# Modulation rows of a hybrid transformer layer: partial sums in four column groups of TensorE

## The chip, the core and the metric

The kernel runs on one core of one Trainium2 chip. A core has four engines that compute, each with a queue of its own that is worked through in order: TensorE (PE in the profile; PEld is its weight load), VectorE (DVE), ScalarE (ACT) and GpSimd (POOL). SyncE (SP) issues the DMA transfers of this kernel, apart from the gathers, which POOL issues. TensorE reads SBUF and writes PSUM, of which there are eight banks of 128 partitions by 512 fp32 values. The metric is the device time of one execution in microseconds (us).

## What is computed

One layer on 512 latent tokens and 256 context tokens of width 1024: a modulated layer norm, a mixing sublayer (windowed attention beside a bidirectional gated delta rule), a second modulated norm, and a product-key retrieval of experts (PEER). The change touches the modulation alone:

```python
mod   = silu(c)     @ w_ada + b_ada          # latent: 6 vectors of 1024
mod_c = silu(c_ctx) @ w_ada + b_ada          # context: the first two are used
sh1, sc1, gt1, sh2, sc2, gt2 = split(mod, 6)
h  = standardize(x) * (1 + sc1) + sh1        # hc likewise, with mod_c
x  = layer_norm(ALPHA * x + gt1 * mixing(h, hc), ln1_g, ln1_b)
h  = standardize(x) * (1 + sc2) + sh2
x  = layer_norm(ALPHA * x + gt2 * peer(h), ln2_g, ln2_b)
```

w_ada is 1024 x 6144 in fp32, 24 MB, so it is read once in full: 24 transfers of 1 MB (half of the 1024 rows, as four k-tiles of 128, by 512 columns).

## The kernel before

The program is written by a planner. Each piece of work is a generator (t_ada1, t_hT, t_qkv, t_prep and so on) that yields, ahead of each instruction, the engine and an estimated duration (p16, p32, dv, ac, pl, dm, lines 164 to 189). The Driver (lines 67 to 153) keeps a time for each engine and emits, among the tasks that could start first, the one with the lowest priority number; it sets the order of every engine's queue. The priorities are in the table X (line 196). A `later` step does not hold its task back. Buffers (SBUF slots, PSUM banks) are taken from and given back to pools, with get and put; seven PSUM banks are one pool (pj, under several names), and the eighth (obk) is another.

The modulation is done in two halves.

The **first half**, t_ada1 (line 506), makes shift and scale of the first norm, for latent and context tokens. For each of four column tiles (ct) and two halves (hf) a 1 MB tile of w_ada is loaded, and four products of a 128x2 stationary operand (silu of c and c_ctx) with 128x512 fp32 values accumulate into two rows of a bank (line 541). The task turn adds the bias on DVE (line 516) and turns the rows into columns with four PE transposes (line 521). When all 16 columns are there, they are copied to modT (lines 549, 551), and t_hT (line 631), which waits for modT, may modulate the transposed tokens (ACT line 643 and DVE line 649) and split them into two fp16 parts (lines 654, 657). All projections read these.

The **second half**, t_ada2 (line 561), makes the four rows for latent tokens that are used later (gt1, sh2, sc2, gt2). Its priority is 9.268, behind the projections of keys, values and queries (3.2 to 6.2) and ahead of the z projections (11.34). It has three slots of SBUF for its 16 loads. It doesn't use TensorE for the sum over the k-tiles: a k-tile is 128 partitions by 512 columns, each partition has one multiplier, and the eight k-tiles are summed elementwise first. Even k-tiles go through DVE (line 611 for the first, 613 after it), odd ones are scaled on ACT (line 604) and added on POOL (lines 607, 617). Then one product with a column of ones sums over the 128 partitions (line 584, in bank obk), DVE adds the bias (line 586), and the row is stored to DRAM (line 590). A column tile ct waits for the store of ct - 2.

When the second half has ended (ev_ada2), the delta rule's recurrence t_chain and its loads t_vin, the attention (t_att0), and two more sets of working buffers become possible, since they use the memory of these slots or read the rows. Before that stand the projections (t_qkv, t_ka, t_qa, t_z: 21 weight tiles of w_in, split into two fp16 parts by ACT line 701 and DVE line 703), the convolution (DVE lines 857 and 860) and the preparation of the delta rule's chunks, t_prep. After the recurrence and the attention follow the output projection t_out (line 1577; its last DVE step on the product is line 1597), and the PEER part: queries (t_q, with DVE line 1802 on its weights), selection and gate matrices (DVE lines 1857 to 2029), and the expert products, which fill TensorE to the end.

## Time and profile before

| | us |
|---|---|
| median of three runs | 1718.34 (1718.12 to 1723.7) |
| profiled execution, its own time | 1715.12 |
| its span, first to last instruction | 1713.3 |

| stretch of the span, us | what runs |
|---|---|
| 0 to 40 | loads, first half of the modulation, statistics of the tokens |
| 40 to 58 | modulated and transposed tokens |
| 58 to 252 | projections, convolution, second half of the modulation, first chunks of the delta rule; the first step of the recurrence on DVE stands at 251.4 |
| 252 to 530 | recurrence, remaining chunks, attention, output projection |
| 530 to 836 | queries of PEER, selection, gate matrices, first expert products |
| 836 to 1713 | expert products |

A busy time is the union of an engine's instructions in a stretch. In the lists by line a group has its count, its busy time and the mean duration of one; durations of neighbours overlap on DVE, ACT and PE, so that busy time by count is nearer to what one more instruction takes. Where an instruction waited, the profile names what ended the wait. The chain of waits follows back from the last instruction to whatever released each one; its shares by line tell on what the end depended. An fp32 product of 512 columns leaves two records on PE, one after the other.

### The profile page before, as it was taken

The numbers are of one execution on the slowest core, as the hardware profiler recorded it, in microseconds if no ns is written. First come the engines' busy times: TensorE is split into PE (matmuls) and PEld (weight loads), VectorE is DVE, ScalarE is ACT, GpSimd is POOL, SyncE is SP. The second block draws the span as 40 slices with busy tenths as digits, with TensorE's granted clock in tenths as the row PEclk, the third lists the DMA queues.
The fourth block names the chain that finished last, engine by engine and source line by source line (L and its number), as shares of the span: only waits on it lengthen the run. The fifth ranks groups of instructions, "written<-read, shape, count | busy, mean of one in ns | idle before, by whom it ended". The sixth has DMA issues, their size and how long they took to land.

```text
span 1713.3 us, 29275 instructions
## 1 busy us (share of the span) xinstructions
PE 1624.7 (95%) x10971; PEld 984.9 (57%) x10971; DVE 1483.8 (87%) x2905; ACT 818.0 (48%) x1475; POOL 530.8 (31%) x383
## 2 busy tenths in 40 slices
PE   8889899888998999999999999999999999989997
PEld 2554466787856885677655555555555555534443
DVE  5789985887899999999987789888888988898976
ACT  2645769777543434566543333333333333344441
POOL 0423451433002000000005455555445545554100
PEclk9999999999999999999999999999999999999999
DMA  9546322222134403599989999999999999999852
GB/s 360 185 156 206 120 75 69 77 66 67 41 133 142 142 2 99 159 271 278 276 302 332 355 353 361 365 375 341 361 381 338 369 361 332 328 344 335 327 182 74
DMA packets 157170, 404.41 MB, mean 236 GB/s; under 512 B 12498, under 2 KB 71378, under 8 KB 151906
## 3 DMA queue, kind: packets, MB, share of 16 engines
q1 hardware_dynamic: 120164, 268.30, 45.5%
q0 software_dynamic: 36864, 134.23, 21.4%
q8 instruction: 86, 1.41, 0.3%
q14 instruction: 56, 0.46, 0.1%
HBM read 365.84 MB, written 36.65 MB: 235 GB/s over the span
## 4 chain that ended last, share of the span: by engine, by line
PE 58%; DVE 29%; issue 5%; ACT 4%; DMA 3%; POOL 1%; SPq 0%; DVEq 0%; POOLq 0%; ACTq 0%
PE bank L207 56%; DVE arena L2101 3%; DVE arena L860 2%; DVE arena L2027 2%; DVE arena L2025 1%; DVE arena L2029 1%; DVE arena L1802 1%; DVE arena L1859 1%; DVE arena L1861 1%; DVE arena L2023 1%; DVE arena L1865 1%; DVE arena L1153 1%; DVE arena L1857 1%; DMA arena<-in_peer_v 1%; DVE arena L1863 1%
## 5 line engine op out<-in xcount | busy, mean ns | idle before, releaser
L207 PE MATMUL bank<-arena 128*128 128x512 f16 (+8 forms) x10490 | 1583.4, 311 | 53.6 <-DVE arena L1153 9.5
L207 PEld LDWEIGHTS <-arena 128*128 128x128 f16 x9528 | 836.7, 98 | 620.9 <-issue 29.0
L2267 POOL DMA_INDIRECT arena<-in_peer_u,arena x128 | 179.7, 1404 | 493.1 <-DVE arena L1975 335.5
L2099 ACT ACTIVATE arena<-arena 128x1024 f16<-128x1024 f32 x128 | 135.1, 1056 | 255.2 <-PE bank L207 211.7
L2267 POOL DMA_INDIRECT arena<-in_peer_v,arena x128 | 194.3, 1518 | 170.7 <-DVE arena L2299 151.5
L2174 ACT ACTIVATE arena<-arena 128x1024 f16<-128x1024 f32 x128 | 134.6, 1052 | 123.2 <-PE bank L207 82.4
L2277 DVE SCALAR_TENSOR_TENSOR arena<-arena 128x1024 bf16<-128x1024 f32 x128 | 156.3, 1221 | 40.0 <-DMA arena<-in_peer_u,arena 37.1
L2176 DVE TENSOR_TENSOR arena<-arena 128x1024 f16<-128x1024 f32 x128 | 156.1, 1220 | 28.7 <-ACT arena L2174 28.3
L2299 DVE SCALAR_TENSOR_TENSOR arena<-arena 128x1024 f32<-128x1024 f32 x126 | 160.4, 1281 | 22.2 <-DMA arena<-in_peer_v,arena 22.1
L2101 DVE SCALAR_TENSOR_TENSOR arena<-arena 128x1024 f16<-128x1024 f32 x128 | 156.5, 1222 | 24.5 <-ACT arena L2099 24.5
L207 PEld LDWEIGHTS bank<-arena 128*128 128x128 f32 (+2 forms) x962 | 114.4, 183 | 49.5 <-issue 31.6
L2195 ACT ACTIVATE arena<-arena 128x384 f16<-128x384 f32 x128 | 66.4, 519 | 157.1 <-DVE arena L2190 148.0
L2041 ACT ACTIVATE arena<-bank 128x512 f32<-128x512 f32 x96 | 55.7, 594 | 40.8 <-PE bank L207 39.1
L2190 DVE TENSOR_TENSOR arena<-arena 128x384 f32<-128x384 f32 x128 | 70.6, 552 | 2.0 <-DMA arena<-wd 2.0
L2197 DVE TENSOR_TENSOR arena<-arena 128x384 f16<-128x384 f32 x128 | 70.6, 551 | 1.3 <-ACT arena L2195 1.3
L607 POOL TENSOR_TENSOR arena<-arena 128x512 f32<-128x512 f32 x24 | 38.2, 1591 | 104.5 <-issue 50.1
L2134 ACT ACTIVATE arena<-bank 128x384 f32<-128x384 f32 x128 | 60.9, 476 | 4.8 <-PE bank L207 4.8
L1111 POOL TENSOR_TENSOR arena<-arena 128x512 f32<-128x512 f32 x12 | 18.2, 1520 | 116.9 <-DVE arena L1108 112.7
L1153 DVE TENSOR_TENSOR arena<-bank,arena 128x512 f16<-128x512 f32 x72 | 48.6, 683 | 4.9 <-PE bank L207 4.7
L860 DVE SCALAR_TENSOR_TENSOR arena<-arena 128x770 f32<-128x770 f32 (+1 forms) x48 | 48.6, 1014 | 0.2
L1572 POOL TENSOR_TENSOR arena<-arena 128x1024 f32<-128x1024 f32 x4 | 11.3, 2830 | 118.3 <-DVE arena L1570 103.7
L1161 ACT ACTIVATE arena<-bank 128x512 f16<-128x512 f32 x60 | 36.4, 611 | 14.7 <-PE bank L207 10.5
(258 smaller groups left out, 1398.5 us busy)
## 6 DMA issues: line engine op xcount, KB each, us to landing
arena<-in_peer_ut SPq DMA_DIRECT2D x128, 512.0 KB
arena<-in_peer_v SPq DMA_DIRECT2D x128, 512.0 KB
arena<-in_w_ada SPq DMA_DIRECT2D x24, 1024.0 KB
wd<-arena SPq DMA_DIRECT2D x24, 1024.0 KB
arena<-wd SPq DMA_DIRECT2D x16, 1536.0 KB
arena<-in_w_int SPq DMA_DIRECT2D x21, 512.0 KB
arena<-in_wq SPq DMA_DIRECT2D x16, 512.0 KB
arena<-in_x SPq DMA_DIRECT2D x8, 512.0 KB
```

The costliest lines, as they stand in the source:

```text
L207: PE.matmul(out, lhsT=l, rhs=r, start=start, stop=stop, skip_group_check=True)
L860: V.scalar_tensor_tensor(acc[:, :n], raw[:, j:j + n], convw[:, ci, j:j + 1], acc[:, :n], op0=OP.mult, op1=OP.add)
L2099: A.activation(hl[0], Ud[e], AF.Copy, scale=US)
L2101: V.scalar_tensor_tensor(hl[1], Ud[e], US, hl[0], op0=OP.mult, op1=OP.subtract)
L2174: A.activation(hl[0], Vd[e], AF.Copy)
L2176: V.tensor_tensor(hl[1], Vd[e], hl[0], op=OP.subtract)
L2190: V.tensor_tensor(a3, a3, Wr[w][:, :, e % 8], op=OP.mult)
L2195: A.activation(g[0], a, AF.Copy)
L2197: V.tensor_tensor(g[1], a, g[0], op=OP.subtract)
L2267: G.indirect_dma_start(out=r, out_offset=None, in_=io[name], in_offset=bass.IndirectOffsetOnAxis(ap=gidx[:, p:p + 1], axis=0))
L2277: V.scalar_tensor_tensor(scr, r, 1.0, h2g, op0=OP.mult, op1=OP.mult, accum_out=gact[:, p:p + 1])
L2299: V.scalar_tensor_tensor(y, r, gact[:, p:p + 1], y, op0=OP.mult, op1=OP.add)
```

## The change

The first half keeps its products, but each of the four k-tiles of a half goes to another quarter of the bank's partitions, 32 columns of the stationary operand wide: sT32[:, 0:8] holds the pair of silu values 16 times over. The four partial rows are then in partitions 0, 32, 64 and 96 (latent) and 1, 33, 65 and 97 (context). ACT copies the whole bank to SBUF, DVE adds the bias to rows 0 and 1, and a product with a 0/1 matrix sel adds the four parts and turns them into columns, in place of the transposes.

The second half does the same in place of the sums on DVE, ACT and POOL: 64 products of 32x512 (a bank of the pool pj is held from the first product to the bias), one copy of the bank on ACT for each ct, one product with sel in place of the one with ones. The planner is told that four such products cost what one costs.

```diff
+    sel = C([2])
-    adacc = [[reg(kb, [512]), reg(90, [512])] for kb in (202.5, 37)]
+    adacc = [reg(kb, [512]) for kb in (202.5, 37)]
+    sT32 = reg(204.5, [16, 32])
 def t_const0():
+        yield dm(1024)
+        sync.dma_start(sel, io["sel"])
         A.activation(sT, cc, AF.Silu)
+        A.activation(sT32[:, 0:8].rearrange("p k (a b) -> p k a b", b=2), sT[:, :, None, :].to_broadcast([128, KT, 16, 2]), AF.Copy)
+        A.activation(sT32[:, 8:16], sT[:, :, 0:1].to_broadcast([128, KT, 32]), AF.Copy)
 def turn(ct, b, ev):
-            V.tensor_tensor(mod1[0:2, ct * 512:(ct + 1) * 512], b[0:2], bA[0:2, ct * 512:(ct + 1) * 512], op=OP.add)
+            yield ac(512)
+            A.activation(mod1[:, cols], b, AF.Copy)
             yield put(pj, b)
+            yield dv(512)
+            V.tensor_tensor(mod1[0:2, cols], mod1[0:2, cols], bA[0:2, cols], op=OP.add)
             yield ev_c1
-                PE.transpose(mps[:, i], mod1[0:2, i * 128:(i + 1) * 128], ident[0:2, 0:2])
+                mm(mps[:, i], mod1[:, i * 128:(i + 1) * 128], sel, True, True)
...
-                yield p32(512, 4)
+                yield p32(512)
                 for k in range(4):
-                    mm(ps[0:2], sT[:, hf * 4 + k], w[:, k], hf + k == 0, hf + k == 4)
+                    s = sT32[:, hf * 4 + k]
+                    mm(ps[32 * k:32 * k + 32], s, w[:, k], hf == 0, hf == 1)
...
 def row(ct, b, ev):
-            b = yield get(obk)
+            acc = adacc[ct % 2]
+            yield ac(512)
+            A.activation(acc, b, AF.Copy)
             yield p32(512)
-            mm(b[0:1], cst[:, C_ONES, 0:1], acc, True, True)
+            mm(b[0:1], sel[:, 0:1], acc, True, True)
             V.tensor_tensor(acc[0:1], b[0:1], bias[0:1], op=OP.add)
-            yield put(obk, b)
+            yield put(pj, b)
 def t_ada2():
-            acc = adacc[ct % 2]
+            b = yield get(pj)
...
+                yield p32(512)
                 for k in range(4):
-                    s = sT[:, hf * 4 + k, 0:1]
-                    if k % 2:
-                        dst = w[:, k] if hf + k > 1 else acc[1]
-                        A.activation(dst, w[:, k], AF.Copy, scale=s)
-                        if hf + k > 1:
-                            G.tensor_tensor(acc[1], acc[1], w[:, k], op=OP.add)
-                    else:
-                        if hf + k == 0:
-                            V.tensor_scalar(acc[0], w[:, k], s, None, op0=OP.mult)
-                        else:
-                            V.scalar_tensor_tensor(acc[0], w[:, k], s, acc[0], op0=OP.mult, op1=OP.add)
+                    s = sT32[:, 8 + hf * 4 + k]
+                    mm(b[32 * k:32 * k + 32], s, w[:, k], hf == 0, hf == 1)
                 yield put(ada, w)
-            G.tensor_tensor(acc[0], acc[0], acc[1], op=OP.add)
...
+    sel[0::32, 0] = sel[1::32, 1] = 1.0
```

No entry of X changes, but the planner's costs do, so it writes another order on every engine. Three places of it follow. In the rows, a name is the line in that kernel's own file, x8 stands for eight equal instructions in a row, and bank_66 to bank_73 are the eight PSUM banks.

The first place is the head of TensorE's queue, before (line 207 is the product, 521 the transposes of a ct, 639 those of the tokens):

```order
L207 MATMUL bank_66<-arena 2x512 x8
L207 MATMUL bank_67<-arena 2x512 x8
L521 MATMUL bank_73<-arena 128x2 x4
L207 MATMUL bank_68<-arena 2x512 x4
L521 MATMUL bank_73<-arena 128x2 x4
L207 MATMUL bank_68<-arena 2x512 x4
L207 MATMUL bank_69<-arena 2x512 x4
L521 MATMUL bank_73<-arena 128x2 x4
L207 MATMUL bank_69<-arena 2x512 x4
L639 MATMUL bank_70<-arena 128x128 x4
```

and after, where the products with sel have line 207 as well, and line 638 has the transposes:

```order
L207 MATMUL bank_66<-arena 32x512 x8
L207 MATMUL bank_67<-arena 32x512 x8
L207 MATMUL bank_73<-arena 128x2 x8
L207 MATMUL bank_68<-arena 32x512 x8
L207 MATMUL bank_73<-arena 128x2 x4
L207 MATMUL bank_69<-arena 32x512 x8
L638 MATMUL bank_70<-arena 128x128 x4
```

The 32 products stay where they were; only the four small ones of a ct stand a little later among them.

The second place is SyncE's queue at the first loads of the second half, before (line 504 loads w_ada, 406 w_in among others, 581 a bias, 590 stores a row, 816 stores keys):

```order
L504 DMA arena<-in_w_ada 128x2048 x2
L406 DMA arena<-in_w_int 128x1024
L504 DMA arena<-in_w_ada 128x2048 x3
L581 DMA arena<-in_b_ada 1x512
L816 DMA ktd<-arena 128x6x128
L504 DMA arena<-in_w_ada 128x2048
L590 DMA modrow<-arena 1x512
L406 DMA arena<-in_w_int 128x1024
L504 DMA arena<-in_w_ada 128x2048
```

and after (511 loads w_ada, 408 w_in, 815 stores keys and values):

```order
L511 DMA arena<-in_w_ada 128x2048 x2
L408 DMA arena<-in_w_int 128x1024
L511 DMA arena<-in_w_ada 128x2048
L815 DMA ktd<-arena 128x6x128
L408 DMA arena<-in_w_int 128x1024 x2
L815 DMA ktd<-arena 128x6x128
L511 DMA arena<-in_w_ada 128x2048
L408 DMA arena<-in_w_int 128x1024 x2
L815 DMA vtd<-arena 128x6x128
L408 DMA arena<-in_w_int 128x1024 x2
```

The loads of the second half have moved behind those of w_in: ahead of the fifth of its 16 loads stand 5 of the 21 tiles of w_in before, and 14 after.

The third place is TensorE's queue near the last rows of the second half. Before, the last row product (into bank_73) follows a projection of z:

```order
L207 LDWEIGHTS arena
L207 MATMUL bank_68<-arena 128x512
L207 MATMUL bank_73<-arena 1x512
L207 LDWEIGHTS arena
L207 MATMUL bank_71<-arena 128x128
```

After, the products of the second half stand there themselves, between small products of the delta rule's chunks (128x128):

```order
L207 MATMUL bank_72<-arena 32x512 x4
L207 MATMUL bank_69<-arena 1x512
L207 MATMUL bank_72<-arena 32x512 x4
L207 LDWEIGHTS arena
L207 MATMUL bank_71<-arena 128x128
```

All 64 of them stand ahead of the recurrence's first product. Counted in the two orders from the last modulated token to the first step of the recurrence, TensorE has 481 products of 128x512 in fp16 after and 417 before, and 212 of 128x128 in fp16 against 146; from there to the last step of the output projection 192 against 255 and 652 against 718, and 199 of 128x256 against 144.

## Rows read from the trace of the kernel before

**Rows 1.** The page, part 1: busy time, share of the span, instructions.

```profile
PE 1624.7 (95%) x10971; PEld 984.9 (57%) x10971; DVE 1483.8 (87%) x2905; ACT 818.0 (48%) x1475; POOL 530.8 (31%) x383
```

**Rows 2.** Busy time by stretch; the first row names the columns.

```profile
core 0: us, PE busy (x) PEld busy (x) DVE busy (x) ACT busy (x) POOL busy (x), PEclk, DMA share, GB/s
0.00:40.00 40.00, 33.57 (x104) 9.07 (x105) 19.86 (x54) 8.43 (x9) 0.45 (x10) 1.00 0.93 369
58.00:120.00 62.00, 52.20 (x366) 33.65 (x365) 48.50 (x87) 35.44 (x84) 21.96 (x14) 0.94 0.53 174
120.00:200.00 80.00, 70.19 (x409) 40.40 (x408) 76.87 (x134) 50.56 (x116) 26.74 (x18) 1.00 0.52 162
200.00:252.00 52.00, 49.03 (x354) 29.45 (x353) 43.51 (x64) 34.58 (x61) 26.24 (x21) 1.00 0.28 95
252.00:530.00 278.00, 253.89 (x2575) 201.45 (x2573) 226.20 (x481) 181.75 (x430) 59.37 (x46) 1.00 0.24 79
530.00:836.00 306.00, 293.80 (x2528) 219.67 (x2526) 305.88 (x949) 158.28 (x297) 11.32 (x4) 0.99 0.55 167
```

**Rows 3.** The chain of waits from 58 to 252 us, shares by line.

```profile
by line: PE bank L207 22.2%; DVE arena L860 15.5%; issue 12.7%; DVE arena L703 4.6%; DMA vtd<-arena 4.2%; DVE arena L613 3.9%; DVE arena L857 3.4%; DVE arena L368 2.8%; ACT arena L864 2.1%; ACT arena L701 2.0%; DVE arena L370 1.8%; DVE aren
```

**Rows 4.** The chain of waits from 252 to 530 us, shares by line.

```profile
by line: PE bank L207 42.7%; issue 5.7%; DVE arena L1153 4.5%; DVE arena L1427 3.6%; ACT arena L1166 2.8%; DVE arena L1391 2.5%; PE bank L1423 2.2%; POOL arena L1111 2.0%; DVE arena L373 1.7%; DVE arena L1802 1.7%; ACT arena L1161 1.6%; DVE
```

**Rows 5.** Times of the recurrence's first and the output projection's last DVE step.

```profile
L1249 DVE TENSOR_TENSOR arena<-bank,arena x12: 675/691/692, 251.4 to 460.0; 128x512 f32<-128x512 f32 x12
...
L1597 DVE SCALAR_TENSOR_TENSOR arena<-bank,arena x8: 636/684/693, 474.0 to 529.7; 128x512 f32<-128x512 f32 x8
```

**Rows 6.** The timeline's start: PE, and the first modulated tokens on ACT.

```profile
6.43 15.36 PE L207 MATMUL bank<-arena 128*2 128x512 f32 x32 [6.43 <-DMA arena<-in_w_ada]
22.06 3.60 PE L207 MATMUL bank<-arena 128*2 128x512 f32 x8
25.92 7.17 PE L207 MATMUL bank<-arena 128*2 128x512 f32 x16
33.35 3.59 PE L207 MATMUL bank<-arena 128*2 128x512 f32 x8
...
37.56 0.67 DVE L516 TENSOR_TENSOR arena<-bank,arena 2x512 f32<-2x512 f32 x1
...
39.63 2.11 ACT L643 ACTIVATE arena<-bank,arena 128x512 f16<-128x512 f32 x3 [0.93 <-DVE arena L551]
```

**Rows 7.** Groups by line and shape, 56 to 230 us: the second half's work.

```profile
L607 POOL TENSOR_TENSOR arena<-arena 128x512 f32<-128x512 f32 x24 | 38.2, 1591 | 104.5 <-issue 50.1 <-ACT arena L604 49.7 <-DVE arena L368 3.6
L604 ACT ACTIVATE arena<-arena 128x512 f32<-128x512 f32 x32 | 22.7, 716 | 5.7 <-POOL arena L617 5.7
L613 DVE SCALAR_TENSOR_TENSOR arena<-arena 128x512 f32<-128x512 f32 x24 | 21.9, 914 | 0.1
L617 POOL TENSOR_TENSOR arena<-arena 128x512 f32<-128x512 f32 x8 | 12.1, 1514 | 2.9 <-issue 1.8 <-POOL arena L607 0.7
L611 DVE TENSOR_SCALAR arena<-arena 128x512 f32<-128x512 f32 x8 | 3.8, 479 | 0.0
```

**Rows 8.** The same list: products that move, and a bank's copy.

```profile
L207 PE MATMUL bank<-arena 128*128 128x512 f16 x378 | 88.1, 379 | 0.0
L207 PE MATMUL bank<-arena 128*128 128x256 f16 x192 | 25.5, 287 | 0.0
L207 PE MATMUL bank<-arena 128*128 128x128 f16 x112 | 8.9, 219 | 2.9 <-DVE arena L1153 2.9
...
L824 ACT ACTIVATE arena<-bank 128x512 f32<-128x512 f32 x11 | 6.5, 590 | 7.2 <-PE bank L207 7.2
```

**Rows 9.** From the timelines of DVE and POOL, 64 to 74 us.

```profile
69.26 1.12 DVE L368 SCALAR_TENSOR_TENSOR arena<-arena 128x6 f32<-128x6 f32 x1
...
71.76 0.17 DVE L368 SCALAR_TENSOR_TENSOR arena<-arena 128x6 f32<-128x6 f32 x1
...
67.45 2.90 POOL L607 TENSOR_TENSOR arena<-arena 128x512 f32<-128x512 f32 x2 [1.92 <-issue]
```

## What the change does to the time: a prediction from these rows

> **What bounds the kernel now.** I read the page first: TensorE is busy 95% of the span, VectorE 87% [rows 1]. The expert products from 836 us on fill TensorE whatever the modulation does, so the change is decided before, and I went by stretches [rows 2]. From 58 to 252 us PE is busy 52.2 + 70.2 + 49.0 = 171.4 of 194 us (idle 22.6), DVE 168.9: two engines near their limit. Inside it, from 120 to 200, DVE is the fuller one (76.9 of 80, PE 70.2). From 252 to 530 PE has 253.9 of 278 (idle 24.1), DVE 226.2; from 530 to 836 DVE is full (305.9 of 306). The chains agree: from 58 to 252 the largest single line is PE's with 22%, but the DVE lines together hold more (860 alone 15.5%, the second half's own line 613 3.9%) [rows 3]; from 252 to 530 PE leads with 43% and the rest are short steps of the chunk ladder [rows 4]. Up to 40 us PE is busy 33.6 us while DMA moves 369 GB/s at a share of 0.93 [rows 2]. So work taken off DVE and POOL can gain only as far as PE has room, and the change puts work on PE.
>
> **The first half, up to 40 us.** Order: unchanged places. The 32 products leave 32 + 8 + 16 + 8 = 64 records in 15.36 + 3.60 + 7.17 + 3.59 = 29.7 us, one after the other almost without a break [rows 6], so PE sets this stage: the last four products run from 33.35 to 36.9, then bias, transposes and the two copies end at 39.6 when ACT takes the first modulated token. With quicker products the loads take over: eight tiles of 1.05 MB and 3.1 MB of tokens at 369 GB/s are 31 us. Behind the last tile come its products (2.25 us, below), a bank's copy on ACT (6.5 us / 11 = 0.59) [rows 8], the bias (0.67) and some 1.3 us for four products and two copies: 35.8. Of these 3.8 us I take 2.5, since the DVE and ACT work on the first weight tiles that now runs inside this wait falls on the modulated tokens instead: **-2.5**, between -4 and +1 (above zero if PE, idle between loads, is granted the lower clock level, which doubles the last products; the granted clock was 0.94 in 58 to 120 us, where PE waits most [rows 2]).
>
> **The second half: taken away.** DVE loses 21.9 + 3.8 = 25.7 us, ACT 22.7, POOL 38.2 + 12.1 = 50.3 [rows 7]. ACT gets eight copies at 0.59, 4.7 us, and is busy 62% there, so these are hidden. POOL's part counts twice: line 368's step of six elements on DVE takes 0.17 us in one place and 1.12 in another, where an addition of line 607 was under way on POOL [rows 9]; I take DVE's relief as 25.7 plus some 10, an estimate.
>
> **The second half: added.** 16 groups of four 32x512 products in fp32. What one group takes is the question, and the trace has no two products in different column groups. Serial, it is eight records: 3.60 us [rows 6]. At best all four run side by side and take what one takes, two records: 0.90. I take a value between, by the order of the records: a product's two records stand 0.45 us apart in the same column group, and PE takes its queue in order. So the second record of one product can run beside the first of the next, which is in another group, but no more: five steps of 0.45 for four products, **2.25**. That is 16 x 2.25 = **36.0 us** on PE, between 14.4 and 57.6. The product with sel replaces the one with ones, at no cost.
>
> The Trainium skill, page TensorE: Matmul & The Clock Gate, section Part 3: Packing small matmuls — row/col tiling, measures three column tiles of 32 at 2.38 times one after the other, and models a pack as one product's time plus 4 ns for each further tile; by it a group here would be near 0.9 us, an estimate, and the sum that of the rival below with four at once. The same section says that matmuls start and end strictly in order, as the pairing above supposes; no row here shows two side by side.
>
> **Moved.** The recurrence needs the second half's end. Before, it was paid for mostly by engines other than PE; now all of it stands ahead in PE's queue, and the planner has also put 64 more 128x512 and 66 more 128x128 fp16 products ahead (the orders in the section on the change): 64 x 88.1/378 + 66 x 8.9/112 = 14.9 + 5.2 = **20.1 us** [rows 8]. They leave the stretch behind, to which 55 products of 128x256 come from later, 55 x 25.5/192 = 7.3 [rows 8].
>
> **The sum.** The recurrence's first DVE step is at 251.4 and the output projection's last at 529.7 [rows 5]; these mark the stretches.
> - 0 to 58: -2.5.
> - 58 to 252: PE needs 171.4 + 36.0 + 20.1 = 227.5 us. Its idle time falls from 22.6, since DVE's load drops from 168.9 to some 133 in a longer stretch; I leave 10 (waits for loads, 12 of the 16 standing close together at 1.05 MB or 2.8 us each, and ladder steps). 237.5 against 194: **+43.5**.
> - 252 to 530: PE loses 20.1 and gets 7.3; its idle time stays, for nothing of the second half stood there: **-12.8**.
> - 530 to 836: DVE-bound, so of the 7.3 us of PE work done early I count about half: **-4** (0 to -7).
>
> Together +24.2 on the profiled execution's 1715.12 (span 1713.3 and 1.8 around it): 1739.3. The median of the runs stands 3.2 above that execution, so 1742.5, and I say **1742**. For this case alone, with the bounds above other than the group's price, 1728 to 1756.
>
> **Rivals.** *One after the other.* If PE doesn't run column groups side by side, a group costs 3.60 and the second half 57.6: 21.6 more, of which I take 4 off as idle time that it fills: **1760**. For it: every record of the trace follows its predecessor; against it: nothing here tries it.
>
> *Four at once.* A group costs 0.90, the second half 14.4: 21.6 less, and PE's idle time rather 12 than 10: **1723**. PE's total then falls (the first half saves some 22 us of records, though loads stand in its way), but the 20.1 us still stand ahead of the recurrence. For it: the planner's figure is no measurement; against it: the order of the records.
>
> *PE's idle time was DVE's and POOL's* (the other side). 22.6 + 24.1 = 46.7 us of idle PE are mostly waits for DVE, ACT and POOL; with four at once and the relief, idle falls to 8 before the recurrence and 12 behind it. Before: 171.4 + 14.4 + 20.1 + 8 = 213.9, +19.9; behind: -12.8 - 12 = -24.8; with -2.5 and -4 that is -11.4: **1707**. It decides from an idle total of 31 us down. For it: DVE at 96% from 120 to 200 us, and waits of tiny steps like that in [rows 9]; against it: behind 252 us none of the removed work ran, so I see no reason for that idle time to fall.
>
> *The change doesn't do what it says*: it does; the orders show the products in four partition groups and no sums on DVE, ACT or POOL. What may fail is only the running side by side, the first rival.
>
> **How the numbers follow.** About 0.5% (8.6 us) is what a measurement of this kernel can tell from no change. Chances: two at a time 0.43, one after the other 0.25, four at once 0.20, idle time gone 0.12. The predicted time is the likeliest case's, 1742. The range takes in most of the last case and of the first rival's upper side: 1707 to 1766, leaving out half of the case at 1707 and a quarter of that at 1760, some 0.15 with the tails. Faster than 1709.7: half of the last case and a little of four at once, 0.10. Within 0.5%, to 1726.9: the rest of the last, most of four at once, a little of the likeliest: 0.22. Slower: 0.68.
>
> **What would show it.** In the profile after: the group's price, from records of 32x512 (x8 in 3.6, 2.25 or 0.9 us); the first modulated token on ACT near 37 us; the recurrence's first step near 293 us (two at a time), 310 (one after the other) or 273 (four at once), with PE over 95% busy between; the output projection's last step 28 us later than now; DVE below 65% in that stretch; the stretch behind shorter by 13. I am wrong if the recurrence starts before 270 us though groups cost over 2 us, or if the stretch behind it changes by more than 20 us.

## The result, and the profile after

The changed kernel takes 1726.47 us (median of six runs, 1724.41 to 1735.17) where the kernel before took 1717.84 beside it (six runs): a ratio of 1.0054, 95% interval 1.0029 to 1.0079. It is slower, as forecast, but by 9 us and not by 24.

Its first profiled execution was the slowest of the six (1735.17). A second set of runs of the same kernel, called **again** below, gave 1729.02 (ratio 1.0053, 1.0036 to 1.0069), and its profiled execution, 1727.85 with a span of 1726.1, is nearer to the median. The rows of "after" here are from that trace. The engines' totals answer to [rows 1]:

```profile
PE 1631.6 (95%) x11115; PEld 993.3 (58%) x11115; DVE 1437.9 (83%) x2873; ACT 798.4 (46%) x1451; POOL 480.9 (28%) x351
```

DVE lost 46 us and POOL 50, and PE gained 7. Two marks of the forecast answer to [rows 5], the recurrence's first step (266.4, before 251.4) and the output projection's last (550.5, before 529.7):

```profile
L1248 DVE TENSOR_TENSOR arena<-bank,arena x12: 675/688/693, 266.4 to 465.4; 128x512 f32<-128x512 f32 x12
...
L1596 DVE SCALAR_TENSOR_TENSOR arena<-bank,arena x8: 681/692/692, 478.2 to 550.5; 128x512 f32<-128x512 f32 x8
```

A third mark turned out more useful than the second: the last step of PEER's gate matrices on DVE. Before:

```profile
L2023 DVE TENSOR_TENSOR arena<-arena x24: 1205/1220/1244, 678.5 to 835.4; 128x2048 f16<-128x2048 f16 x24
```

and after:

```profile
L2022 DVE TENSOR_TENSOR arena<-arena x24: 1198/1216/1223, 692.0 to 848.8; 128x2048 f16<-128x2048 f16 x24
```

From there to the end of the span it is 877.9 us before and 877.3 after, and 874 to 888 in every trace of this study: but for that spread, the end is decided at this mark. Busy time between the marks (columns as in [rows 2]), of before:

```profile
58.00:251.40 193.40, 170.82 (x1124) 103.19 (x1123) 168.28 (x282) 119.98 (x261) 74.34 (x52) 0.98 0.46 148
251.40:529.70 278.30, 254.19 (x2577) 201.48 (x2575) 226.54 (x480) 182.23 (x430) 59.97 (x46) 1.00 0.24 79
529.70:835.40 305.70, 293.50 (x2528) 219.60 (x2526) 305.54 (x949) 158.18 (x298) 11.32 (x4) 0.99 0.55 166
```

and of after:

```profile
58.00:266.40 208.40, 201.37 (x1404) 114.90 (x1401) 133.83 (x265) 115.89 (x254) 22.27 (x19) 1.00 0.43 144
266.40:550.50 284.10, 249.98 (x2520) 204.55 (x2521) 226.43 (x509) 168.98 (x419) 61.69 (x47) 0.97 0.23 74
550.50:848.80 298.30, 285.74 (x2455) 213.14 (x2453) 296.60 (x914) 154.45 (x288) 7.98 (x3) 0.99 0.56 168
```

Three things are to be seen. Ahead of the recurrence PE is now full (idle 7.0 us where it was 22.6) and DVE is not (idle 74.6, before 25.1). From the recurrence to the output projection the stretch is 5.8 us longer although no work was added: PE's idle time grew from 24.1 to 34.1, and its granted clock fell from 1.00 to 0.97. Behind that DVE is full in both (idle 0.2 and 1.7). Sum: +15.0 + 5.8 - 7.4 = +13.4 at the third mark. The two spans differ by 12.8 and the medians by 9, since the profiled execution of before lies some 3 us below the median of its runs.

### The profile page after: what moved, and what is told of

Read it like the earlier page. It is cut to its first block, busy times and chain, and to the rows that moved or that the text cites. A ratio compares the mean times of both kernels' runs of the same rounds, so it can differ in the third digit from the quotient of the medians.

```text
span 1733.4 us, 29451 instructions
## 1 busy us (share of the span) xinstructions
PE 1635.5 (94%) x11115; PEld 991.9 (57%) x11115; DVE 1436.7 (83%) x2873; ACT 798.5 (46%) x1451; POOL 482.9 (28%) x351
## 4 chain that ended last, share of the span: by engine, by line
PE 51%; DVE 20%; DMA 13%; issue 9%; ACT 4%; POOL 3%; SPq 0%; POOLq 0%; DVEq 0%; ACTq 0%
PE bank L207 49%; DMA arena<-in_peer_v,arena 8%; POOL arena L2266 3%; DVE arena L2100 3%; DVE arena L2026 2%; DVE arena L2024 1%; DVE arena L2028 1%; DMA arena<-in_w_ada 1%; DMA arena<-in_peer_v 1%; DVE arena L2022 1%; DMA arena<-in_w_out 1%; DVE arena L2298 1%; DVE arena L1152 1%; DVE arena L1858 1%; DVE arena L1801 1%
## 5 line engine op out<-in xcount | busy, mean ns | idle before, releaser
L207 PE MATMUL bank<-arena 128*128 128x384 f16 (+7 forms) x10650 | 1592.6, 318 | 67.4 <-DMA arena<-in_w_ada 13.6
L2266 POOL DMA_INDIRECT arena<-in_peer_u,arena x128 | 175.8, 1374 | 490.9 <-DVE arena L1974 329.8
L2266 POOL DMA_INDIRECT arena<-in_peer_v,arena x128 | 203.5, 1590 | 168.9 <-DVE arena L2298 146.8
L2298 DVE SCALAR_TENSOR_TENSOR arena<-arena 128x1024 f32<-128x1024 f32 x126 | 160.5, 1280 | 36.1 <-DMA arena<-in_peer_v,arena 35.8
L207 PEld LDWEIGHTS bank<-arena 128*128 128x128 f32 (+1 forms) x1122 | 118.8, 180 | 51.6 <-issue 19.1
L1110 POOL TENSOR_TENSOR arena<-arena 128x512 f32<-128x512 f32 x12 | 16.1, 1345 | 225.3 <-DVE arena L1107 209.4
L1152 DVE TENSOR_TENSOR arena<-bank,arena 128x512 f16<-128x512 f32 x72 | 48.8, 686 | 18.3 <-PE bank L207 16.8
L1160 ACT ACTIVATE arena<-bank 128x512 f16<-128x512 f32 x60 | 36.4, 609 | 22.3 <-PE bank L207 21.9
L859 DVE SCALAR_TENSOR_TENSOR arena<-arena 128x770 f32<-128x770 f32 (+1 forms) x48 | 44.3, 928 | 0.7
L1165 ACT ACTIVATE arena<-bank 128x512 f16<-128x512 f32 x60 | 36.5, 611 | 14.2 <-PE bank L207 13.6
```

The lines of the kernel that those rows point to most:

```text
L207: PE.matmul(out, lhsT=l, rhs=r, start=start, stop=stop, skip_group_check=True)
L1152: V.tensor_tensor(p, tp, b4(m16[:, d * 7 + l]), op=OP.mult)
L2266: G.indirect_dma_start(out=r, out_offset=None, in_=io[name], in_offset=bass.IndirectOffsetOnAxis(ap=gidx[:, p:p + 1], axis=0))
L2298: V.scalar_tensor_tensor(y, r, gact[:, p:p + 1], y, op0=OP.mult, op1=OP.add)
```

## The experiments

Each was run beside the kernel before on the same chip, but not all on one chip, so rows are compared by their ratios (0.1% is 1.7 us); "recurrence" is its first DVE step in the run's trace.

| run | median us | ratio to before (95%) | recurrence |
|---|---|---|---|
| first_only | 1717.57 | 0.9990 (0.9980 to 1.0001) | 251.6 |
| one_group | 1766.02 | 1.0268 (1.0243 to 1.0292) | 306.9 |
| half_products | 1728.30 | 1.0054 (1.0033 to 1.0076) | 260.8 |
| sums_in_new_order | 1758.75 | 1.0244 (1.0210 to 1.0277) | 296.1 |
| both_old_costs | 1738.80 | 1.0108 (1.0087 to 1.0129) | 278.5 |
| second_sums_old_costs | 1736.02 | 1.0104 (1.0080 to 1.0129) | 276.6 |
| ad2_5 | 1728.03 | 1.0050 (1.0034 to 1.0067) | 266.3 |
| sums_back_unused | 1746.97 | 1.0162 (1.0135 to 1.0188) | 289.8 |
| dve_back_unused | 1740.12 | 1.0117 (1.0085 to 1.0148) | 275.6 |
| pool_back_unused | 1730.40 | 1.0054 (1.0039 to 1.0070) | 269.7 |
| o2_13 | 1726.16 | 1.0036 (1.0023 to 1.0048) | 266.8 |
| gap_filled | 1735.22 | 1.0098 (1.0066 to 1.0130) | 266.5 |
| retuned | 1706.82 | 0.9920 (0.9904 to 0.9936) | 242.1 |
| retuned_2 | 1725.18 | 1.0045 (1.0030 to 1.0060) | 210.5 |
| retuned_3 | 1718.33 | 0.9999 (0.9987 to 1.0012) | 239.3 |
| retuned_sums | 1746.47 | 1.0153 (1.0123 to 1.0183) | 279.5 |
| before_new_table | 1733.86 | 1.0071 (1.0046 to 1.0096) | 250.4 |

**The kernel again.** 

> The changed kernel itself, unaltered, for a second profile. Its first profiled execution took 1735.2 us, 8.7 above the median of its runs (1726.5), and in that trace PE stood idle some 10 us more than before behind 1200 us, in expert products that the change doesn't touch. If that is chance, the median is again 1725 to 1729, this profile is nearer to it, and PE's idle time behind 1200 us is that of before (some 6 us from 1200 to 1600, where the first profile had 15). If it belongs to the new order, it stands there again. The recurrence's first DVE step near 266 us, the output projection's last near 549, in either case.

Chance: PE's idle time from 1200 to 1600 us is 5.4 us (before 4.5; in the first profile 9.1), and the end 877 us behind the third mark (886 in the first profile). These are smaller than the figures that I expected, and say the same.

**What a group costs.** Groups by line and shape up to the recurrence, after (count, busy time, mean duration of one record):

```profile
L207 PE MATMUL bank<-arena 128*32 128x512 f32 x128 | 18.3, 603 | 0.0
```

The 128 records are 603 ns long and take 18.3 us together, so four run at a time: 1.14 us for a group, against 3.60 for eight records one after the other [rows 6]. One group alone, from the timeline:

```profile
159.50 1.07 PE L207 MATMUL bank<-arena 128*32 128x512 f32 x8
```

and what of it is still under way from 160.5 us on, the second records of the four products, side by side:

```profile
159.95 0.61 PE L207 MATMUL bank<-arena 128*32 128x512 f32 x4
```

In one_group the four go into one column group, in the same order of instructions:

```diff
-                    mm(b[32 * k:32 * k + 32], s, w[:, k], hf == 0, hf == 1)
+                    mm(b[0:32], s, w[:, k], hf + k == 0, hf + k == 4)
```

> The changed kernel, same order on every engine, but the four products of a group of the second half accumulate in one column group (partitions 0 to 31), so none can run beside another; copy and row product then take 32 partitions. In the changed kernel's trace a group's four products start 6 ns apart and a group takes 0.43 us twice with 0.1 to 0.2 around it. Expected of the group here: eight records 0.43 to 0.45 us apart, 3.6 us, so 16 x 2.5 = 40 us more on PE ahead of the recurrence. Theory B (PE sets that stretch, and what it gets there comes on the end in full): recurrence near 305, total 1762 to 1772. Rival (waits for loads and other engines absorb a part of it): recurrence before 295, total 1740 to 1755.

```profile
L207 PE MATMUL bank<-arena 128*32 128x512 f32 x128 | 57.7, 595 | 0.0
```

57.7 - 18.3 = 39.4 us more on PE; the recurrence came 40.5 later and the median rose by 37. What is added on PE there comes on the end nearly in full. Taking away is another matter. half_products leaves out the second group of each row:

```diff
-                for k in range(4):
+                for k in range(4 * hf, 4):
-                    mm(b[32 * k:32 * k + 32], s, w[:, k], hf == 0, hf == 1)
+                    mm(b[32 * k:32 * k + 32], s, w[:, k], True, True)
```

> The changed kernel in the same order, but of the two groups of each row of the second half the second is left out, so the rows are those of half the k-tiles: 8 groups fewer, some 9 us less on PE ahead of the recurrence; loads, copies, row products stay. Theory B (PE sets the stretch): recurrence 8 to 10 us earlier, near 257, total 1716 to 1720. Rival (rows and ladder steps set it, the products lie in gaps): recurrence within 3 us of 266, total 1724 to 1729.

The first two stretches of half_products:

```profile
58.00:260.80 202.80, 193.76 (x1338) 113.51 (x1335) 133.73 (x265) 115.71 (x254) 22.25 (x19) 1.00 0.44 149
260.80:546.60 285.80, 249.73 (x2520) 204.78 (x2521) 226.94 (x509) 169.26 (x419) 61.62 (x47) 0.97 0.24 74
```

PE was busy 7.6 us less, the recurrence came 5.6 earlier, the third mark 3.1 earlier, and the median 0.7, which is nothing beside the noise. The stretches behind the recurrence are longer by 1.7, 0.8 and (from the third mark on) 2.0 us; what in them took the gain isn't shown. Theory B's total failed; the rival's came, though the recurrence moved further than it allowed.

**The first half alone.** Of the diff, the parts in t_const0, turn and t_ada1, with the planner's old costs, so that every queue keeps its order.

> The first half of the modulation alone as in the change (32 products in four column groups, bank copied by ACT, product with sel), with every engine's order as in the kernel before and the second half as before. Theory A (loads and the lower clock take the first half's gain): PE has 20 us less to do up to 40 us, but the last tile of weights sets the end; PE idles between loads, its products run at the lower of the two clock levels, and the transposes that follow too: the first modulated token 0 to 1.5 us earlier, the first DVE step of the recurrence within 3 us of 251.4, total 1715 to 1720. Rival (the first half gains as forecast): first modulated token 2.5 us earlier and all behind it: 1714 to 1716, and the changed kernel's loss lies in its second half alone. Second rival: the lower clock lasts into the projections and costs more than is gained: 1720 to 1723.

Even (-0.9 us, within the noise), though PE is busy 25.0 us up to 40 us and not 33.6. The timeline of first_only (start, duration) shows why:

```profile
32.21 3.50 ACT L495 ACTIVATE arena<-arena 128x1024 f32<-128x1024 f32 x3 [3.36 <-DVE arena L503]
...
36.56 0.57 ACT L522 ACTIVATE arena<-bank 128x512 f32<-128x512 f32 x1
...
38.56 1.87 PE L207 MATMUL bank<-arena 128*128 128x2 f32 x8 [0.20 <-DVE arena L523]
...
40.82 2.79 ACT L650 ACTIVATE arena<-bank,arena 128x512 f16<-128x512 f32 x4 [0.38 <-DVE arena L558]
```

The last bank's copy (L522), a step that the change adds on ACT, stands in ACT's queue behind the standardizing of the tokens (L495), which waited for the statistics on DVE, and behind one split of weights. The last group of products was done near 35.5 (before 36.9); but the bias on DVE had to wait for the copy, the products with sel took 1.87 us, and the first modulated token (L650) came at 40.8, later than before (39.6). Between the loads PE rests, and its groups here take 1.9 us, not 1.1 (below).

In the changed kernel's own order the start looks better, and ends the same way. In again the first modulated token is at 37.9, 1.7 us earlier than before, near the forecast's mark of 37. But the last of them starts on DVE at 53.0 (line 648; before 52.2, line 649): the lead is lost within the stage. The granted clock is 0.66 there from 40 to 50 us, where PE is busy 6.6 of 10 us, and 1.00 in the kernel before; what it has to do with the loss isn't shown.

**Instructions or order.** The change does two things: it exchanges instructions, and it makes the planner write another order. sums_in_new_order keeps the changed kernel's order and does the second half's sums as before, at the products' places:

```diff
                 yield p32(512)
-                for k in range(4):
-                    s = sT32[:, 8 + hf * 4 + k]
-                    mm(b[32 * k:32 * k + 32], s, w[:, k], hf == 0, hf == 1)
+                for k in range(4):
+                    (the steps of DVE, ACT and POOL of the kernel before, with no yields)
```

> The order of the changed kernel, with its first half, but the second half's sums done as before on DVE, ACT and POOL at the places where the four products stand; the row product with ones. So against the changed kernel it is the second half's instructions alone. Theory A: PE loses 18 us of products, DVE gets 26 us, ACT 18, POOL 50 in the same stretch, where the sums stand close together (12 of the 16 late): the rows wait for POOL, the recurrence starts 5 to 20 us later than the 266.6 of the changed kernel, total 1732 to 1748. Rival (PE bounds this stretch, DVE and POOL have room): the 18 us come off, recurrence near 250, total 1708 to 1716.

Same order, old sums: 30 us slower than the changed kernel, in an order whose planner knew nothing of the sums. Of PE's waits up to the recurrence (total, times, longest) the first two, there:

```profile
PE bank L207 <- DVE arena L1162: 18.1, 6, 5.9
PE bank L1184 <- ACT arena L1180: 7.4, 1, 7.4
```

both_old_costs is the opposite, the change in an order planned with the old costs, and second_sums_old_costs does the old sums in that order. The yields of the kernel before stay, and behind the join stand the products:

```diff
                     if k % 2:
                         yield ac(512, 1, 1)
-                        A.activation(dst, w[:, k], AF.Copy, scale=s)
...
                 yield ("join",)
+                for k in range(4):
+                    mm(b[32 * k:32 * k + 32], sT32[:, 8 + hf * 4 + k], w[:, k], hf == 0, hf == 1)
```

> The whole change, but planned with the costs of the kernel before: the planner still counts the old steps on DVE, ACT and POOL for the second half, and the four products are put where the fourth of those steps stood; the partial rows gather in the bank that the row products had (taken from the first product on, which shifts the plan a little). Theory A (the instructions gain, the new order loses what they gain): the second half's work is early again, PE's idle time ahead of the recurrence falls by some 15 us against 18 us of new products, and the stretch behind keeps its cover: recurrence near 250, total 1705 to 1715, that is faster than before and by over 10 us than the changed kernel. Rival (PE is the bound, the order has no part in it): 18 us of products come on top of PE's work ahead of the recurrence whatever the order: 1722 to 1732, as the changed kernel.

> The order of the run both_old_costs (1738.8, recurrence at 278.5), with its first half, but the second half's sums on DVE, ACT and POOL as in the kernel before, at the planner's places for them. So the difference to both_old_costs is the second half's instructions alone, in an order that was made for the sums. Theory B (PE has no room; the relief of DVE and POOL is worth something only where the rows wait for them): the products cost here what they take, 16 to 18 us, less the waits that go: this one 1722 to 1732, 7 to 17 faster than both_old_costs. Rival (the products gain as in the changed kernel's order, 30 us against the sums): this one 1755 to 1770. If it comes out near 1738, the instructions are even and the whole loss of both_old_costs is its order.

Up to the recurrence, the products and then the sums:

```profile
58.00:278.50 220.50, 205.10 (x1393) 114.88 (x1392) 137.31 (x269) 118.92 (x258) 24.36 (x19) 0.98 0.44 140
```

```profile
58.00:276.60 218.60, 192.04 (x1263) 115.17 (x1262) 173.06 (x301) 134.22 (x282) 73.17 (x51) 0.97 0.44 141
```

13.1 us more on PE and 35.8 less on DVE, and the end is even (ratios 1.0108 and 1.0104): PE's idle time falls by 11 and pays for nearly all of the products. So theory A fell: the old costs do not help the change. But both runs are 16 to 20 us behind the kernel before, whose sums are the same as in the second run: a small shift of the plan (one bank is taken earlier) costs more than the whole change. So the change in the order of the kernel before itself was not run.

**The place of the second half.** ad2_5 changes one number of the planner's table:

```diff
-X = {... 'ad2': 9.268, ...}
+X = {... 'ad2': 5.0, ...}
```

> The changed kernel with one number of the planner's table changed: the priority of the second half, 9.268, becomes 5.0, ahead of the projections that it now competes with on PE; the planner writes a new order. In the changed kernel the first row is stored at 154 us (before: 84), the last at 259. Theory C (the rows come late because the products stand behind the projections, and the ladder behind the recurrence then lacks work to fill PE's waits): rows from about 85 on, the last before 235, recurrence near 250, PE's idle time from the recurrence to the output projection's end back to some 45 us from 58: total 1712 to 1720. Rival (PE's sum of work is what counts, wherever the products stand): 1724 to 1730.

The rows' stores, after and then in ad2_5:

```profile
L603 SPq DMA_DIRECT2D modrow<-arena x8: 215/242/243, 158.9 to 259.4; - x8
```

```profile
L603 SPq DMA_DIRECT2D modrow<-arena x8: 222/242/281, 76.8 to 141.8; - x8
```

The rows are all done 118 us earlier, and the recurrence starts at 266.3 as before it. Theory C fell: the rows do not set its start. That PE's sum of work ahead of it does (198.4 busy of 208.3 us there, 201.4 of 208.4 in the changed kernel) fits, but is argued.

**What the relief is worth.** In sums_back_unused the products stay, and steps on DVE and POOL that nothing reads are put beside them:

```diff
+                for k in range(0, 4, 2):
+                    V.scalar_tensor_tensor(scr[0], w[:, k], sT[:, hf * 4 + k, 0:1], w[:, k], op0=OP.mult, op1=OP.add)
+                    G.tensor_tensor(scr[1], w[:, k + 1], w[:, k + 1], op=OP.add)
```

> The changed kernel in its own order; beside each group of the second half two steps of DVE and two of GpSimd on the same weights, as many and as wide as the sums that the change took away (32 each), whose results nothing reads; ACT's scaling isn't put back. It tells what the relief of DVE and GpSimd is worth in this order. DVE gets some 26 us, GpSimd some 45, before the recurrence. Theory B (PE sets this stretch, the relief is worth little): recurrence 0 to 4 us later, total 1728 to 1733. Rival (PE's waits come from DVE and GpSimd, the last rival of the prediction): recurrence 8 us later or more, total 1736 or more.

The two that follow have the line on V or the line on G alone.

> As the run sums_back_unused (1747.0, 19 us above the changed kernel, recurrence at 289.8), but only DVE's 32 unused steps are put back, 32.7 us there, not GpSimd's. In the changed kernel DVE is idle 78 us from 40 to 266. If GpSimd's relief is what counts (its steps stand ahead of the chunks' own additions in its queue): 1727 to 1732, recurrence within 4 us of 266. If DVE's counts: 1738 to 1746. If both share it: 1733 to 1738.

> As the run sums_back_unused, but only GpSimd's 32 unused steps, 42 us there, not DVE's. In that run PE stood still 5.0 us at 221 and 5.5 at 248 for DVE steps of the chunks that waited for GpSimd's addition (line 1110 of the changed kernel), which stood behind four of the unused steps, 6 to 7.5 us. If GpSimd's queue is what counts: 1740 to 1747, recurrence near 286 to 290, the same two gaps. If DVE's load counts: 1727 to 1732.

By ratio, against the changed kernel's 1.0053: both +19 us, DVE's alone +11, POOL's alone nothing that the noise would show. The steps stand in for the sums and aren't the same: DVE's take about what the sums took there (24.7 us alone, 25.7 before), ACT's scaling isn't put back, and each tile of weights is held until they are done. DVE's 32 steps alone and, in the second fence, with POOL's beside them:

```profile
L618 DVE SCALAR_TENSOR_TENSOR arena<-arena 128x512 f16<-128x512 f32 x32 | 24.7, 771 | 0.6
```

```profile
L618 DVE SCALAR_TENSOR_TENSOR arena<-arena 128x512 f16<-128x512 f32 x32 | 32.7, 1023 | 0.6
```

So DVE's relief counts, and POOL's mostly through DVE, whose steps last a third longer beside it. This although DVE idles 75 us there: its steps stand between PE's. PE's waits up to the recurrence with both back, the longest first:

```profile
PE bank L207 <- DVE arena L1156: 9.4, 4, 5.5
PE bank L207 <- DVE arena L1182: 5.8, 2, 5.0
```

In the changed kernel the wait of the first row (its line 1152) is 1.7 us. PE's idle time up to the recurrence is 23.6 us with both back, 7.0 without. So the rival with PE's idle time due to DVE and POOL was right ahead of the recurrence (7.0 us of idle time for its 8), and wrong behind it (34.1 for its 12).

**The gap in the tail.** PE's timeline after, near 500 us:

```profile
496.67 4.10 PE L207 MATMUL bank<-arena 128*128 128x128 bf16 x39
507.68 1.11 PE L1422 MATMUL bank<-arena 128*128 128x128 f32 x4 [6.91 <-ACT arena L1404]
```

The transposes of the last attention tile (its exponentials are line 1404) come in PE's queue when nothing else is left ahead of them. From 500 to 510 us, where PE stood still, the granted clock is 0.67, from 510 to 520 it is 0.82 (1 stands for 2.4 GHz, 0.5 for 1.2). o2_13 leaves the output projection of token tile 2 for that place, and gap_filled puts in products that serve nothing:

```diff
-X = {... 'o2': 11.022, ...}
+X = {... 'o2': 13.0, ...}
```

> The changed kernel with one other number of the planner's table: the priority of the output projection of token tile 2, 11.022, becomes 13.0, just behind the attention of token tile 3 (12.86), so that its products are left to run while that attention waits. In the changed kernel's traces PE stands still for 6.9 us near 500 (transposes of tile 3's first head wait for the exponentials on ACT), 1.7 near 508 and 4.7 near 575, and is then granted the lower clock for 10.2 and 6.8 us, half the speed: 13.3 + 8.5 = 21.8 us; the kernel before has 2.6 + 1.7 there. Theory D (the loss against the kernel before lies in this tail, not in the products): both long gaps go, 10 to 14 us come back, total 1714 to 1719, recurrence unmoved near 266. Rival (the stretch behind is full of DVE work that starts no earlier, or the gap moves to the next attention step): 1723 to 1729.

```diff
             tp = bk(b, [4, 128])
+            if (i, s, t) == (3, 0, 0):
+                for _ in range(28):
+                    mm(b, ident16, m16[:, 0:4].rearrange("p a b -> p (a b)"), True, True)
             yield ptr32(4)
```

> The changed kernel in its own order, with 28 products of 128x512 in fp16 that serve nothing put in front of the transposes of tile 3's first head, where PE stands still 6.9 us: 28 x 0.216 = 6.0 us. They don't shorten the wait; they tell what the lower clock behind it costs. If the clock falls because PE stood still: no lower clock at 503 to 513, and of the 5.1 us that it cost there 3 to 5 come back: total 1723 to 1726 against 1727 to 1729. Rival (the granted clock falls there for another reason, or the work behind waits for DVE anyway): total unchanged at 1727 to 1729, or 2 later where the filling outlasts the wait.

o2_13, second and third stretch:

```profile
266.80:533.30 266.50, 238.03 (x2450) 193.62 (x2451) 214.50 (x453) 164.38 (x410) 59.32 (x46) 1.00 0.24 75
533.30:845.90 312.60, 296.54 (x2519) 219.46 (x2517) 310.13 (x969) 155.86 (x296) 11.25 (x4) 0.99 0.55 164
```

The gap and the lower clock are gone (1.00), the output projection ends 17 us earlier, and the third mark moves by 2.9: the stretch behind is longer by 14. Theory D fell too. DVE's work of both stretches together is nearly the same (524.6 us, 523.0 in the changed kernel); 13.5 us of it now stand behind the mark, where DVE is busy 310.1 of 312.6. The likely reason stands beside the gap. The row of the changed kernel from 500 to 510 us:

```profile
500.00:510.00 10.00, 1.88 (x12) 1.16 (x9) 9.98 (x32) 1.37 (x3) 0.00 (x0) 0.67 0.25 100
```

While PE stands still, DVE is busy 9.98 of 10 us, with norms and steps of the attention that are needed anyway. gap_filled missed its aim, as its timeline shows (25 of its 28 products have a record):

```profile
507.90 8.42 PE L207 MATMUL bank<-arena 128*128 128x512 f16 x25 [6.91 <-ACT arena L1404]
```

The filling itself waited for the exponentials, whose bank it had been given; it came behind the gap and cost 6 to 8 us in full. What the clock alone costs there stays open.

**An order made for the change.** The old table of priorities was made for the old costs. retuned, retuned_2 and retuned_3 are the changed kernel with three other tables, which a search over the planner's own estimate gave; the instructions are the same. Some entries of the first:

```diff
-X = {'ch': 6.003, 'ka': 8.11, 'ad2': 9.268, 'a2': 9.456, 'a3': 12.86, 'o2': 11.022, ...}
+X = {'ch': 9.826, 'ka': 4.188, 'ad2': 8.735, 'a2': 6.911, 'a3': 10.535, 'o2': 12.544, ...}
```

> The changed kernel with another table of priorities: the old table was made for the costs of the kernel before, this one for those of the change. By the planner's own figures it ends 31 us before the changed kernel's plan and 4 behind that of the kernel before, and it leaves no gap over 2.1 us on PE from 60 us to the expert products, where the changed kernel's has 7.2 and 4.5. Theory D: the gaps and the low clock at 500 and 575 go, 12 to 20 us: total 1708 to 1717, level with the kernel before or a little faster. Rival (16 to 18 us of products are on PE now and must be paid): 1720 to 1730.

> The changed kernel with a second table of priorities, found independently of that of retuned; the planner's own end is 6 us later than that one's (1666 against 1660; kernel before 1656, changed kernel 1691). If orders made for the change gain in general: 1705 to 1716, recurrence before 255. If retuned was one lucky order: 1718 to 1730.

> As retuned_2 with a third table; the planner's own end is 3 us later than that of retuned. If orders made for the change gain in general: 1703 to 1714. If retuned was one lucky order: 1718 to 1730.

The three stretches of retuned:

```profile
58.00:242.10 184.10, 179.09 (x1319) 106.37 (x1318) 128.75 (x242) 108.98 (x243) 26.56 (x21) 1.00 0.47 158
242.10:517.20 275.10, 254.09 (x2528) 200.79 (x2528) 220.21 (x485) 179.05 (x427) 56.19 (x44) 0.99 0.25 80
517.20:824.10 306.90, 294.79 (x2531) 220.19 (x2531) 306.01 (x949) 159.66 (x299) 10.28 (x4) 0.99 0.56 167
```

Against the changed kernel PE has 22.3 us less to do ahead of the recurrence and 4.1 more behind it, where its idle time is 21.0, not 34.1. It beats both kernels, the one before by 0.8%, and is faster than either theory said. But the two other tables gave +0.45% and no difference, while the planner's figures for the three lie within 6 us. retuned_2 starts the recurrence at 210.5 and pays for it behind:

```profile
210.50:525.30 314.80, 289.99 (x2718) 221.53 (x2718) 244.02 (x507) 200.41 (x465) 70.12 (x55) 0.99 0.25 78
```

So an early recurrence is no gain by itself, and one order of three being better is no proof that such orders are better in general. Two controls tell the table from the change: retuned's order with the old sums at the products' places, and the kernel before with the new table and nothing else changed.

> The order of the run retuned (1706.8, recurrence at 242.1), with its first half, but the second half's sums on DVE, ACT and GpSimd as in the kernel before, at the places of the products. So the difference to retuned is the second half's instructions alone in an order that suits the change. In the changed kernel's order the same exchange cost 30 us (1758.8 against 1728), in an order made for the sums it gained 3 (1736.0 against 1738.8). Theory E (the products are cheap where the order is made for them): 1725 to 1740. Rival (the table made the gain, whatever the instructions): 1700 to 1712.

> The kernel before, its planner given the table of the run retuned; the planner makes its own order for the old sums. Theory E (the gain of retuned comes from the change with an order made for it; the old table is the better one for the old sums): 1720 to 1735. Rival (the new table is the better one whatever the instructions, and the change gains nothing by itself): 1700 to 1712.

The old sums in retuned's order are 40 us slower than its products, and the kernel before, planned with that table, is 14 us slower than with its own. Neither table nor instructions gain alone; the pair does. But three tables were searched for the change and none for the old sums, so it isn't shown that the change beats old sums with a table sought for them now.

## Why the forecast was too high, by its own steps

The direction and the range were right; the size was not, 24 us for 9. By the marks, the stretch up to the recurrence was forecast at +41 and came at +15.0, the next at -12.8 and came at +5.8, the third at -4 and came at -7.4. The two large errors have opposite signs, so the total is nearer than the steps.

- **First half (-2.5): wrong, about 0.** The step "loads take over" held: PE waits for loads between its groups. The steps behind the last tile were mis-sized. The forecast had the copy on ACT as its 0.6 us alone and left out ACT's queue, where it stands behind work that waits for the statistics (first_only). In the changed kernel the first modulated token does come 1.7 us earlier, and the last 0.8 later.
- **Group (36.0 for 16): the step that made the forecast too high.** I let only the second record of one product run beside the first of the next. In fact four run at once: 18.3 us. The page TensorE: Matmul & The Clock Gate of the Trainium skill, section Part 3: Packing small matmuls — row/col tiling, has a pack as one product's time plus some ns for each further tile; an estimate from that model is 0.9 us, and the trace is near it with 1.07 us for a group. I had it beside the sum and took the rows' order for a reason against it; order at the start and end of records doesn't keep them from overlapping.
- **Moved (20.1 ahead of the recurrence): right.** The two shapes that it named take 112.3 + 18.1 us there after and 95.8 + 12.2 before, 22.4 more. PE's whole busy time grew by 30.6, 18.3 of it the groups and 12.3 the rest, since other shapes got less (and the granted clock went from 0.98 to 1.00).
- **Idle (10 left of 22.6): near**, 7.0.
- **Behind the recurrence (-12.8): wrong in sign, +5.8.** The step "its idle time stays" failed: it rose by 10.0, and 6.9 of it is the one wait near 500 us (below 1.7 us is every single wait of before in this stretch). PE's busy time fell by 4.2 only (254.2 to 250.0), with the granted clock at 0.97 for 1.00. That the work that moved ahead had been the filling is argued.
- **530 to 836 (-4): near**, -7.4, and in o2_13 this DVE-bound stretch gave 14 of the 17 us gained ahead of it back.

The rival "four at once" with 1723 was the case that came, with a group's price as it said. That its total is only 3 to 6 us low is in part luck: by its own terms the stretch up to the recurrence comes at +21.4 (measured +15.0), the next at -12.8 (+5.8). My last rival was the same case with idle time that falls; sums_back_unused shows that such relief is worth 19 us in this order. Where it went is not settled: into 18 us of products and into work that the new order put ahead, so I argue, but half_products, with half of those products gone, is no faster. Shown: the price of a group, the worth of the relief in this order, that the rows' time doesn't set the recurrence. Not settled: how much of the 9 us is the order's chance. Seven orders of the change gave 1707 to 1739 us, five of the old sums 1718 to 1759. The spread of the orders is wider than the change.

## What to carry to other kernels

Where a planner rewrites the order with a change, measure the instructions in a fixed order and the order with fixed instructions, each apart: here the same exchange of instructions was worth 30 us in one order, 40 in another and nothing in a third, the order alone as much, and the change as a whole 9. Work taken off an engine with idle time can still be worth part of its duration if its steps stand between those of the full engine (here 11 us for 24.7 of DVE's); unused work put back shows it at once. Before filling a gap on one engine, see what the engine that is full later does in it: here it worked through the gap, and filling it moved the end by 3 us.

## What was not expected of the hardware

- Four fp32 products of 128x512 with 32 columns each, in four column groups: eight records in 1.07 us, against 3.60 one after the other, 3.4 times.
- A DVE step with two SBUF inputs took 0.77 us and, with additions on POOL put beside it, 1.02 (32 of each). The Trainium skill, page SBUF — State Buffer, section Who interferes with whom, has such a step contend with POOL's reads; the trace agrees.
- At the start of the span PE runs at half its speed although the granted clock of 0 to 30 us reads 1.00: the first group takes 1.94 us, against 1.07 at 159.5, and so do those behind each wait for a load. The 32 records from 18.20 are two groups with the small products of sel between them, without a break, and the second of these groups (23.57) still takes 1.93:

```profile
6.81 1.94 PE L207 MATMUL bank<-arena 128*32 128x512 f32 x8 [6.81 <-DMA arena<-in_w_ada]
10.54 1.93 PE L207 MATMUL bank<-arena 128*32 128x512 f32 x8 [1.80 <-DMA arena<-in_w_ada]
...
18.20 7.30 PE L207 MATMUL bank<-arena 128*32 128x512 f32 x32 [1.85 <-DMA arena<-in_w_ada]
```

The kernel before starts slowly too, and goes faster soon: its first four records take 3.35 us, 0.84 each, and the other 28 of the 32 that run without a break [rows 6] some 12.0, 0.43 each. What keeps the changed kernel slow for longer, no run here separates.

```profile
6.43 3.35 PE L207 MATMUL bank<-arena 128*2 128x512 f32 x4 [6.43 <-DMA arena<-in_w_ada]
```
